# Query and key rotation in eight dealt steps, and a PSUM ring turned by one bank, in a transformer layer on one core

## The chip, the cores and the metric

The kernel runs on one core of a Trainium2 chip. It is one launch that computes a whole layer for 512 latent tokens and 128 context tokens, 640 in all. The metric is the device time of one execution in microseconds (us). The kernel before takes 1811.43 us, the median of three runs from 1809.01 to 1812.48 us.

The core has five engines with a queue each. PE multiplies matrices and writes its sums to PSUM, a memory of eight banks. DVE does arithmetic on two tensors and reductions. ACT does functions of one tensor, copies among them. POOL and SP issue most of the transfers here. Each engine works through its own queue in order and waits for the others by semaphores.

## The reference

A layer is a half-step feed-forward block, then two token mixers side by side (differential attention and a chunked linear recurrence, the mLSTM), a gated sum of the two, and a second half-step feed-forward block. The change touches the attention branch. What is computed there:

```python
dq = rmsnorm(dq.reshape(B, T, DA_HEADS, 2, DA_HEAD_DIM), p['g_qn'][l])
dk = rmsnorm(dk.reshape(B, T, DA_HEADS, 2, DA_HEAD_DIM), p['g_kn'][l])
q_att = rope_2d(dq)                                   # latent tokens only
keys  = concatenate([rope_2d(dk), k_ctx])
s  = einsum('bqhcd,bkhcd->bhcqk', q, k) * scale
pr = softmax(s)                                       # c = 0, 1
w  = pr[:, :, 0] - lam * pr[:, :, 1]
out = einsum('bhqk,bkhv->bqhv', w, v)
```

Each query and each key is a vector of 64. It is divided by its root mean square, scaled by a gain and, for the 512 latent tokens, rotated: each pair (x1, x2) becomes (x1 cos - x2 sin, x2 cos + x1 sin). The 128 context tokens get norm and gain alone, and their keys are also an output (`new_k`). There are eight heads of two vectors each, and attention has a pair of softmaxes per head.

## The kernel before, in words

The token axis lies in five tiles of 128: four of latent tokens and one of context tokens. Matrix products are in fp32r with every operand split into a high and a low part, three products for one (`mm3`). Weights come in granules of 1 MB, are loaded to `raw`, and are split by one ACT copy (`wH`, the high part) and one DVE subtraction (`wL`, the low part).

**The prelude** (from about 450 to 650 us of the span) makes the queries and keys of pair 0, that is of heads 0 and 1, and then twelve granules of gates. Its PSUM pool `ps2` has five banks under one tag, `mm`. Groups of token tiles take one bank each (`tok_group`), and each of the twelve granules takes three (X, Y and Z, in `products`). Then the pool is closed and its five banks are given to two new pools, `ps2m` with four banks and `ps2w` with one; a tile of the new pools waits until the old tile in its place has been read.

**The attention blocks** (about 684 to 1061 us) are 8 heads x 5 query tiles, in two loops in lines 2035 and 2037: head `hd`, query tile `qi`. A block does, in the order of the program:

1. `scores(qi)`: PE multiplies the query tile by all keys into the PSUM tile `sc`, and DVE takes the row minimum (`mn`);
2. `turn(qi-1)`: PE transposes the weights of the query tile before (`ps_wT`), and ACT copies them out (`wT`);
3. `soft(qi)`: ACT takes two exponentials of `sc`;
4. `aside(hd, qi, 0)`: one pending low part of a weight granule, if there is one (`fill.low()`);
5. one unit of other work for PE (`fill.units`), to cover the softmax;
6. `mix(qi)`: DVE joins the two softmaxes (`rc`, `r`, `p`);
7. `values(qi-1)`: PE multiplies the turned weights by the values (`ps_o`), and DVE scales them (`ao`);
8. in query tile 3, `pack` of the next head: ACT copies `qpk`, `kpk`, `kpk`, and DVE a subtraction `qpk`;
9. `aside(hd, qi, 1)`, perhaps a second unit of other work, and `fill.ahead()`, which loads and splits weights to come.

After the fifth block a tail turns the last query tile, transposes the next head's queries and keys (`ps_qkT`), does three units, and ends with `finish_norm` of the head's result. The transposes of that result (`ps_aT`, in `finish`) come in the first block of the next head.

The units of other work come from a queue, `fill`. A unit of a token granule makes one tile of 128 tokens; a unit of a wide pair (two granules side by side, ten units) makes half of one and uses the single bank of `ps2w`; a unit of a feature granule makes a quarter of a transposed product. The queue's order before is: values 0, keys 1, queries 1, wide values 1 and memory values 0, wide keys 2 and queries 2, memory queries 1 (feature), wide values 2, wide keys 3 and queries 3, wide values 3, then feature granules. The numbers are pairs of heads: pair 2 is heads 4 and 5. `UNITS` says how many units each block takes: 2, 1, 2, 1, 1 and three in the tail for most heads.

**What sets the order.** PE instructions stay in program order (`mm`, `tr`). For the other engines a planner runs a model of the chip and issues what it finds ready, except inside `with written():`. There each ACT or DVE instruction is chained behind the previous written one of its engine, so the written instructions of an engine form one row in the order of the program (`placed`, lines 37 to 47). Instructions outside are put between them by the planner. Steps 1, 2, 3, 4, 6, 7, 8 and `fill.ahead()` above are written.

**Norm and rotation before** (`qk_norm_rope`, line 1530) is called when the last tile of a projection of queries or keys has been copied out. It is not written: the planner puts its instructions where it finds room. It squares (ACT), sums (DVE), takes the inverse root (ACT logarithm and exponential, three small DVE instructions), multiplies (DVE), copies with halves swapped (ACT), multiplies by the sine and by the cosine table, adds, and multiplies the context tile by the gain (DVE).

Of the kernel before, what the change touches and what calls it, by code (L numbers as in the profile page):

```python
# [7 lines left out]
F32 = mybir.dt.float32  # L8
F32R = mybir.dt.float32r
BF16 = mybir.dt.bfloat16  # L10
AF = mybir.ActivationFunctionType
# [20 lines left out]
def tile_trunk(ctx: ExitStack, tc: tile.TileContext, a: dict):  # L32
# [17 lines left out]
    def act(*args, **kw):  # L50
        return placed(nc.scalar.activation(*args, **kw))  # L51

    def tt(eng, out, in0, in1, op):
        return placed(eng.tensor_tensor(out=out, in0=in0, in1=in1, op=op))  # L54
# [4 lines left out]
    def ts(out, in0, s1, op0, s2=None, op1=None):  # L59
        if s2 is None:  # L60
            placed(vec.tensor_scalar(out=out, in0=in0, scalar1=s1, scalar2=None, op0=op0))
        else:
            placed(vec.tensor_scalar(out=out, in0=in0, scalar1=s1, scalar2=s2, op0=op0, op1=op1))
# [4 lines left out]
    @contextmanager  # L68
    def written():
        was, as_written[0] = as_written[0], in_row  # L70
        yield
        as_written[0] = was
# [107 lines left out]
    def rstd_of(pool, ss, inv_n, shape, tag, bufs=1, ytag=None, ybufs=1):  # L180
        v = pool.tile(shape, F32, tag=tag + "v", name="rv", bufs=bufs)
        y = pool.tile(shape, F32, tag=ytag or tag + "y", name="ry", bufs=max(bufs, ybufs))
        t = pool.tile(shape, F32, tag=tag + "t", name="rt", bufs=bufs)
        ts(v, ss, inv_n, ALU.mult, EPS, ALU.add)
        act(t, v, AF.Ln)
        act(y, t, AF.Exp, scale=-0.5)
        newton_rsqrt(y, v, t)
        return y
# [1334 lines left out]
    def rope_place(of):  # L1523
        if not late_p:
            return rope_p[0].tile([128, 5, 256], F32, tag="pk", name="rope", bufs=2)
        return late_p[0].tile([128, 5, 256], F32, tag="rope", name="rope")

    at_rope = [None]

    def qk_norm_rope(raw, tab):  # L1530
        A, B, g = tab
        sq = rope_place("q")
        act(sq, raw, AF.Square)
        ss = rope_p[0].tile([128, 20], F32, tag="ss", name="ss", bufs=2)
        vec.tensor_reduce(out=ss, in_=sq.rearrange("p t (g d) -> p (t g) d", d=64), axis=AX.X, op=ALU.add)
        rs = rstd_of(rope_p[0], ss, 1.0 / 64, [128, 20], "qk")
        r3 = raw.rearrange("p t (g d) -> p (t g) d", d=64)
        tt(vec, r3, r3, rs[:, :, None].to_broadcast([128, 20, 64]), ALU.mult)
        sw = rope_place("k")[:, 0:4]
        at_rope[0] = act(  # L1540
            sw.rearrange("p t (b s j) -> p (t b) s j", s=2, j=16),
            raw[:, 0:4, :].rearrange("p t (b s j) -> p (t b) s j", s=2, j=16)[:, :, ::-1, :],
            AF.Copy,
        )
        s4 = sw.rearrange("p t (g d) -> p t g d", d=64)
        q4 = raw[:, 0:4, :].rearrange("p t (g d) -> p t g d", d=64)
        tt(vec, s4, s4, B[:, :, None, :].to_broadcast([128, 4, 4, 64]), ALU.mult)
        tt(vec, q4, q4, A[:, :, None, :].to_broadcast([128, 4, 4, 64]), ALU.mult)
        tt(vec, raw[:, 0:4, :], raw[:, 0:4, :], sw, ALU.add)
        p3 = raw[:, 4, :].rearrange("p (g d) -> p g d", d=64)  # L1550
        tt(vec, p3, p3, g[:, None, :].to_broadcast([128, 4, 64]), ALU.mult)

    q_tok, k_tok, v_tok = {}, {}, {}

    def project_q(pr, now=lambda f: f()):
        def make():
            q_tok[pr] = t = (ap if pr % 2 else qk).tile([128, 5, 256], F32, tag="qtok", name="q_tok")

            def evac(p, i):
                act(t[:, i, :], p, AF.Copy)  # L1560
                if i == 4:
                    now(lambda: qk_norm_rope(t, tabs[0]))

            return evac

        return a["w_dq"][pr], make

    def project_k(pr, now=lambda f: f()):
        def make():
            t = (ap if pr % 2 else qk).tile([128, 5, 256], F32, tag="ktok", name="k_tok")  # L1570
            k_tok[pr] = t

            def evac(p, i):
                act(t[:, i, :], p, AF.Copy)
                def whole():
                    qk_norm_rope(t, tabs[1])
                    nc.sync.dma_start(out=a["new_k"][:, pr * 256 : (pr + 1) * 256], in_=t[:, 4, :])

                if i == 4:
                    now(whole)  # L1580

            return evac

        return a["w_dk"][pr], make

    def project_v(pr):
        def make():
            v_tok[pr] = t = ap.tile([128, 7, 256], F32, tag="vtok", name="v_tok", bufs=2)
            nc.sync.dma_start(out=t[:, 4:6, :], in_=a["cache_v"][:, :, pr * 256 : (pr + 1) * 256])

            def evac(p, i):
                act(t[:, i if i < 4 else 6, :], p, AF.Copy)
                if i == 4:
                    nc.sync.dma_start(out=a["new_v"][:, pr * 256 : (pr + 1) * 256], in_=t[:, 6, :])

            return evac

        return a["w_dv"][pr], make
# [192 lines left out]
    def wide(*projects):  # L1791
        fill.pair([src for src, _ in projects], lambda: wide_units(psum, [make() for _, make in projects]))

    def queries_of_memory(h):
        def evac(p, mt, hf):
            t = ap.tile([128, HALF], F32, tag="stage", name="stage", bufs=2)
            act(t, p, AF.Copy, scale=0.0625)
            nc.sync.dma_start(out=mq_dram[:, 2 * h + mt, half(hf)], in_=t)
        feature(a["w_mq"][h], lambda: evac)

    def keys_of_memory(h):
        def evac(p, mt, hf):
            t = ap.tile([128, HALF], F32, tag="stage", name="stage", bufs=2)
            vec.tensor_copy(t, p)
            nc.sync.dma_start(out=mk_dram[:, 2 * h + mt, half(hf)], in_=t)
        feature(a["w_mk"][h], lambda: evac)
# [8 lines left out]
    def memory_values(h):  # L1815
        return a["w_mv"][h], lambda: v_evac(h)
# [7 lines left out]
    token(project_q(1))  # L1824
    wide(project_v(1), memory_values(0))
    projections(2)
    queries_of_memory(1)
    wide(project_v(2), memory_values(1))
    projections(3)
    wide(project_v(3), memory_values(2))  # L1830
    keys_of_memory(1)
    queries_of_memory(2)
    keys_of_memory(2)
# [85 lines left out]

    heads = [Head(hd) for hd in range(8)]  # L1920
    gates = ExitStack()
    tok_group(psum, [(w_q, i, e_q) for i in (2, 3, 4)], lambda k: None)
    G.work[0][0].load()
    with tc.issue_after(box["normed"]):
# [93 lines left out]
    def aside(hd, qi, part):  # L2018
        if hd == 0:
            for _ in range(ROWS.get((qi, part), 0)):  # L2020
                next(rows, None)
        if part == 0:
            with written():
                fill.low()
        if part == 1 and hd == 1 and qi in (1, 2):
            gate_load(qi - 1)
        if part == 0 and hd == 1 and qi in (2, 3):
            gate_cols()
# [5 lines left out]
    late = None  # L2034
    for hd in range(8):
        H = heads[hd]
        for qi in range(5):
            n = UNITS[hd][qi]
            with written():
                H.scores(qi)  # L2040
                if qi > 0:
                    H.turn(qi - 1)
                H.soft(qi)
            aside(hd, qi, 0)
            fill.units(n[0])
            with written():
                H.mix(qi)
            if late is not None:
                late()
                late = None  # L2050
            if qi > 0:
                with written():
                    H.values(qi - 1)
            if qi == 3 and hd < 7:
                with written():
                    heads[hd + 1].pack()
            aside(hd, qi, 1)
            if (hd, qi) == (0, 2):
                begin_pools()
            fill.units(n[1])  # L2060
            with written():
                fill.ahead()
        n = UNITS[hd][-1]
        with written():
            H.turn(4)
        if hd < 7:
            N = heads[hd + 1]
            N.queries()
            fill.units(n[0])
            with written():  # L2070
                H.values(4)
            H.finish_norm()
            N.keys(0)
            fill.units(n[1])
            N.keys(1)
            with written():
                fill.ahead()
            fill.units(n[2])
            late = H.finish
        else:  # L2080
            fill.eager = True
            fill.units(1)
            H.values(4)
            H.finish_norm()
            fill.drain(3)
            with written():
                H.finish()
# [547 lines left out]
```

## Time and profile before

| what | us |
|---|---|
| three runs, lowest, median, highest | 1809.01, 1811.43, 1812.48 |
| the profiled execution's own time | 1810.32 |
| its span, first to last instruction | 1808.4 |
| PE busy in the span | 1778.9 |
| DVE busy | 1346.6 |
| ACT busy | 900.2 |

The profile is of one execution. An instruction's row gives its start in us from the start of the span, its duration, engine, line, operation, the tiles it writes and reads, and shapes; in brackets stands the time for which its engine sat idle just before it, and who ended that wait. PE instructions overlap: a product of 128 x 512 starts 0.23 us after the one before it and yet is shown with about 0.4 us. So a busy PE is not a PE at its peak, and an idle time under 0.15 us gets no bracket. DVE and ACT instructions overlap by some 0.05 to 0.1 us.

### The profile page before, as it was taken

How to read it: one execution, taken by the hardware profiler on the slowest of the kernel's cores; microseconds unless marked ns; L12 is line 12 of the kernel's file. 1: busy time of each engine (PE TensorE's matmuls, PEld its weight loads, DVE VectorE, ACT ScalarE, POOL GpSimd, SP SyncE). 2: the span in 40 equal slices, each digit the busy share in tenths (PEclk: the TensorE clock that was granted, in tenths of full speed). 3: DMA queues.
4: the chain of work that ended last, by engine and by line, in shares of the span. 5: the costliest groups of instructions: out<-in, count | busy, mean ns of one | idle time of the engine just before them, and what ended most of it. 6: DMA issues, size and time to landing. Idle time of an engine off the chain costs nothing.

```text
span 1808.4 us, 29656 instructions
## 1 busy us (share of the span) xinstructions
PE 1778.9 (98%) x11950; PEld 1713.3 (95%) x11950; DVE 1346.6 (74%) x2162; ACT 900.2 (50%) x1579; POOL 41.0 (2%) x72
## 2 busy tenths in 40 slices
PE   8999999999999999999999999999999999999998
PEld 7999999999999999898889998899999999999998
DVE  6889987677988768667586447877668888897475
ACT  5654544333655456554565447562326545554432
POOL 0000000100000000000000000000000000000010
PEclk9999999999999999999999999999999999999999
DMA  8355566978245533312223335665652455557992
GB/s 325 114 198 173 185 236 220 351 223 272 84 138 183 195 129 100 110 61 69 75 72 110 106 99 197 188 244 205 217 173 77 134 173 187 203 180 272 355 311 84
DMA packets 144923, 317.85 MB, mean 176 GB/s; under 512 B 10577, under 2 KB 106577, under 8 KB 133009
## 3 DMA queue, kind: packets, MB, share of 16 engines
q1 hardware_dynamic: 133410, 270.20, 43.9%
q0 software_dynamic: 10688, 43.13, 7.4%
q10 hardware_dynamic: 688, 2.63, 0.4%
q8 instruction: 94, 1.54, 0.3%
q14 instruction: 43, 0.35, 0.1%
HBM read 243.77 MB, written 72.15 MB: 175 GB/s over the span
## 4 chain that ended last, share of the span: by engine, by line
PE 84%; DVE 8%; DMA 5%; ACT 2%; issue 1%; SPq 0%; DVEq 0%; ACTq 0%
PE ps_f L75 48%; PE ps_p L75 14%; PE ps_t L75 11%; PE sc L75 3%; PE ps_o L75 2%; PE ps_n L75 2%; DVE ww L54 2%; DMA raw_a<-in_w_ada_k 1%; PE ps_wT L78 1%; DMA P<-nm_dram 1%; PE ps_u L75 1%; PE ps_qkT L78 1%; DVE junk L814 1%; DMA raw<-in_w2b 1%; DMA a_raw<-aT_dram 1%
## 5 line engine op out<-in xcount | busy, mean ns | idle before, releaser
L75 PE MATMUL ps_f<-S,ww 128*128 128x320 f32 x2400 | 387.0, 309 | 3.2 <-DMA S<-g_dram 1.0
L75 PEld LDWEIGHTS ps_f<-S,ww 128*128 128x128 f32 x2400 | 359.8, 188 | 7.2 <-DVE ww L54 4.6
L54 DVE TENSOR_TENSOR ww<-raw,ww 128x2048 fp32r<-128x2048 f32 (+1 forms) x73 | 163.9, 2245 | 65.5 <-ACT ww L51 65.4
L75 PE MATMUL ps_f<-hm,ww 128*128 128x320 f32 x1176 | 185.6, 309 | 0.1
L75 PEld LDWEIGHTS ps_f<-hm,ww 128*128 128x128 f32 x1176 | 175.7, 188 | 0.3 <-DVE ww L54 0.3
L51 ACT ACTIVATE ww<-raw 128x2048 fp32r<-128x2048 f32 (+1 forms) x73 | 136.8, 1875 | 57.1 <-DVE raw L54 37.8
L54 DVE TENSOR_TENSOR raw<-raw 128x1024 f32<-128x1024 f32 x186 | 160.7, 864 | 2.4
L75 PE MATMUL ps_f<-hm,wB 128*128 128x320 f32 x1008 | 161.5, 309 | 0.0
L75 PE MATMUL ps_t<-wH,hH 128*128 128x256 f32 (+1 forms) x440 | 151.4, 344 | 2.9 <-DVE g_out L54 1.5
L75 PE MATMUL ps_p<-hH,wH 128*128 128x320 f32 x480 | 151.1, 315 | 1.6 <-DVE num L54 1.4
L75 PEld LDWEIGHTS ps_f<-hm,wB 128*128 128x128 f32 x1008 | 151.3, 188 | 0.0
L75 PE MATMUL ps_p<-hH,wL 128*128 128x320 f32 x480 | 148.3, 309 | 0.0
L75 PE MATMUL ps_p<-hL,wH 128*128 128x320 f32 x480 | 148.3, 309 | 0.0
L75 PE MATMUL ps_t<-wH,hL 128*128 128x256 f32 (+1 forms) x440 | 146.7, 333 | 0.9 <-DVE hL L54 0.9
L75 PE MATMUL ps_t<-wL,hH 128*128 128x256 f32 (+1 forms) x440 | 146.2, 332 | 0.0
L51 ACT ACTIVATE u<-ps_f 128x320 f32<-128x320 f32 x129 | 55.8, 433 | 157.0 <-PE ps_f L75 156.9
L51 ACT ACTIVATE wH<-raw 128x2048 fp32r<-128x2048 f32 (+1 forms) x45 | 75.4, 1683 | 48.8 <-PE ps_p L75 37.3
L54 DVE TENSOR_TENSOR wL<-raw,wH 128x2048 fp32r<-128x2048 f32 x37 | 84.6, 2286 | 19.5 <-ACT wH L51 19.3
L1674 DVE TENSOR_REDUCE mn<-sc 128x2 f32<-128x1536 f32 (+1 forms) x40 | 59.6, 1490 | 50.2 <-PE sc L75 50.0
L54 DVE TENSOR_TENSOR wB<-raw,wB 128x1024 fp32r<-128x1024 f32 x64 | 78.0, 1219 | 24.4 <-ACT wB L51 24.4
L814 DVE CUSTOM_DVE_ANT_0 junk<-raw_a,csil 128x1024 bf16<-128x1024 f32 (+1 forms) x76 | 92.5, 1217 | 2.1 <-DMA raw_a<-in_w_ada_c 1.6
L75 PEld LDWEIGHTS ps_t<-wH,hH 128*128 128x128 f32 x440 | 83.6, 190 | 11.0 <-DVE g_out L54 1.7
(306 smaller groups left out, 3595.9 us busy)
## 6 DMA issues: line engine op xcount, KB each, us to landing
g_dram<-g SPq DMA_DIRECT2D x44, 640.0 KB, 7.6
raw_a<-in_w_ada_c POOLq DMA_DIRECT2D x38, 512.0 KB, 5.1
g_dram<-g SPq DMA_DIRECT2D x24, 480.0 KB, 8.4
raw<-in_w1b SPq DMA_DIRECT2D x11, 1024.0 KB, 5.0
raw<-in_w3b SPq DMA_DIRECT2D x11, 1024.0 KB, 6.2
raw<-in_w1a SPq DMA_DIRECT2D x10, 1024.0 KB, 5.0
raw<-in_w3a SPq DMA_DIRECT2D x10, 1024.0 KB, 6.2
hm<-g_dram SPq DMA_DIRECT2D x7, 1280.0 KB, 11.8
```

The lines of the kernel that those rows point to most:

```text
L51: return placed(nc.scalar.activation(*args, **kw))
L54: return placed(eng.tensor_tensor(out=out, in0=in0, in1=in1, op=op))
L75: tc.keep_in_program_order(nc.tensor.matmul(*args, **kw))
L78: tc.keep_in_program_order(nc.tensor.transpose(*args, **kw))
L814: placed(vec.tensor_tensor_reduce(out=junk, in0=raw, in1=self.csil[:, v, :], op0=ALU.mult, op1=ALU.add, scale=1.0, scalar=0.0, accum_out=m ...
L1674: placed(vec.tensor_reduce(out=mn, in_=sv, axis=AX.X, op=ALU.min))
```

## The change

It does four things.

- `qk_norm_rope` becomes `rope_steps`, a list of eight functions: `square` (ACT), `sums` (DVE: reduction and a small scaling), `root` (two small ACT instructions), `divide` (three small DVE instructions and a product), `swap` (ACT), `by_sine` (DVE), `by_cosine` (DVE), `add` (DVE: the sum and the gain of the context tile; then the store of `new_k` for keys). The instructions are those of before. Pair 0 still runs them in one go.
- For pairs 1 to 3 the finished projection appends its list to `rotations`. A new function `rotate` runs the next step of the first list, and under some conditions also one of the second, inside `written()`, so that the steps take places in the rows of ACT and DVE. It is called in `aside` part 0 if `fill.low()` had nothing to do, in `aside` part 1 always, after the block's second units if two lists are open, and, in query tile 3 of odd heads, until nothing is left, ahead of `pack` of the next head.
- `queries_of_memory(1)`, a feature granule of four units, moves in the fill queue from behind the wide pair of keys 2 and queries 2 to behind wide values 3.
- In the prelude, ahead of the second group of queries, a PSUM tile `ps_turn` is taken from `ps2` and never used.

```diff
-    def qk_norm_rope(raw, tab):
+    def rope_steps(raw, tab, then=lambda: None):
         A, B, g = tab
...
+        def sums():
...
+            placed(vec.tensor_reduce(out=ss, in_=box.pop("sq").rearrange("p t (g d) -> p (t g) d", d=64), axis=AX.X, op=ALU.add))
+            ts(box["v"], ss, 1.0 / 64, ALU.mult, EPS, ALU.add)
+        def root():
+            act(box["t"], box["v"], AF.Ln)
+            act(box["y"], box["t"], AF.Exp, scale=-0.5)
+        def divide():
+            newton_rsqrt(box["y"], box["v"], box["t"])
+            r3 = raw.rearrange("p t (g d) -> p (t g) d", d=64)
+            tt(vec, r3, r3, box["y"][:, :, None].to_broadcast([128, 20, 64]), ALU.mult)
...
+        return [square, sums, root, divide, swap, by_sine, by_cosine, add]
+
+    def qk_norm_rope(*args):
+        for f in rope_steps(*args):
+            f()
+
+    rotations = []
+
+    def rotate():
+        if not rotations:
+            return False
+        first, second = rotations[0], rotations[1] if len(rotations) > 1 else []
+        had, left = len(first), len(second)
+        with written():
+            if not (had == 4 and left == 7):
+                first.pop(0)()
+            if left == 8 and had in (5, 6) or left in (5, 6, 7) and left >= had + 2 or left == 7 and had == 4:
+                second.pop(0)()
+            if not first:
+                rotations.pop(0)
+        return True
...
-                    now(lambda: qk_norm_rope(t, tabs[0]))
+                    if now:
+                        now(lambda: qk_norm_rope(t, tabs[0]))
+                    else:
+                        rotations.append(rope_steps(t, tabs[0]))
...
     projections(2)
-    queries_of_memory(1)
     wide(project_v(2), memory_values(1))
     projections(3)
     wide(project_v(3), memory_values(2))
+    queries_of_memory(1)
     keys_of_memory(1)
...
+    psum.tile([128, 512], F32, tag="mm", name="ps_turn")
     tok_group(psum, [(w_q, i, e_q) for i in (2, 3, 4)], lambda k: None)
...
         if part == 0:
             with written():
-                fill.low()
+                split = fill.low()
+            if not split:
+                rotate()
+        else:
+            rotate()
...
+        odd = hd % 2
...
             if qi == 3 and hd < 7:
+                while odd and rotate():
+                    pass
                 with written():
                     heads[hd + 1].pack()
             aside(hd, qi, 1)
...
             fill.units(n[1])
+            if len(rotations) > 1:
+                rotate()
             with written():
                 fill.ahead()
```

More of the change, by code (lines that the diff above doesn't have):

```diff
@@ L1528, in tile_trunk @@
     at_rope = [None]
-    def qk_norm_rope(raw, tab):
+    def rope_steps(raw, tab, then=lambda: None):
         A, B, g = tab
[L1532 to L1551, printed above, removed]
@@ new lines, in rope_steps, with square @@
+        box = {}
+        def square():
+            box["sq"] = rope_place("q")
+            act(box["sq"], raw, AF.Square)
+        def sums():
+            box["v"], box["t"], box["y"], ss = (
+                rope_p[0].tile([128, 20], F32, tag="qk" + n, name="qk" + n, bufs=2) for n in ("v", "t", "y", "ss")
+            )
+            placed(vec.tensor_reduce(out=ss, in_=box.pop("sq").rearrange("p t (g d) -> p (t g) d", d=64), axis=AX.X, op=ALU.add))
+            ts(box["v"], ss, 1.0 / 64, ALU.mult, EPS, ALU.add)
@@ new lines, in root, with swap @@
+        def root():
[5 more added lines that the diff above has]
+            tt(vec, r3, r3, box["y"][:, :, None].to_broadcast([128, 20, 64]), ALU.mult)
+        def swap():
+            box["sw"] = rope_place("k")[:, 0:4]
+            at_rope[0] = act(
+                box["sw"].rearrange("p t (b s j) -> p (t b) s j", s=2, j=16),
+                raw[:, 0:4, :].rearrange("p t (b s j) -> p (t b) s j", s=2, j=16)[:, :, ::-1, :],
+                AF.Copy,
+            )
@@ new lines, in by_sine, with by_cosine, add @@
+        def by_sine():
+            s4 = box["sw"].rearrange("p t (g d) -> p t g d", d=64)
+            tt(vec, s4, s4, B[:, :, None, :].to_broadcast([128, 4, 4, 64]), ALU.mult)
+        def by_cosine():
+            q4 = raw[:, 0:4, :].rearrange("p t (g d) -> p t g d", d=64)
+            tt(vec, q4, q4, A[:, :, None, :].to_broadcast([128, 4, 4, 64]), ALU.mult)
+        def add():
+            tt(vec, raw[:, 0:4, :], raw[:, 0:4, :], box["sw"], ALU.add)
+            p3 = raw[:, 4, :].rearrange("p (g d) -> p g d", d=64)
+            tt(vec, p3, p3, g[:, None, :].to_broadcast([128, 4, 64]), ALU.mult)
+            then()
@@ L1553, in tile_trunk, with project_q @@
     q_tok, k_tok, v_tok = {}, {}, {}
-    def project_q(pr, now=lambda f: f()):
+    def project_q(pr, now=None):
         def make():
@@ L1561, in evac, with project_k @@
                 if i == 4:
-                    now(lambda: qk_norm_rope(t, tabs[0]))
+                    if now:
+                        now(lambda: qk_norm_rope(t, tabs[0]))
+                    else:
+                        rotations.append(rope_steps(t, tabs[0]))
             return evac
         return a["w_dq"][pr], make
-    def project_k(pr, now=lambda f: f()):
+    def project_k(pr, now=None):
         def make():
@@ L1574, in evac, with store @@
                 act(t[:, i, :], p, AF.Copy)
-                def whole():
-                    qk_norm_rope(t, tabs[1])
+                def store():
                     nc.sync.dma_start(out=a["new_k"][:, pr * 256 : (pr + 1) * 256], in_=t[:, 4, :])
                 if i == 4:
-                    now(whole)
+                    if now:
+                        now(lambda: qk_norm_rope(t, tabs[1], store))
+                    else:
+                        rotations.append(rope_steps(t, tabs[1], store))
             return evac
@@ L2023, in aside @@
             with written():
-                fill.low()
+                split = fill.low()
+            if not split:
+                rotate()
+        else:
+            rotate()
         if part == 1 and hd == 1 and qi in (1, 2):
```

## The prediction

> **What bounds the kernel now.** First the page: busy times and the chain that ended last.
>
> ```profile
> PE 1778.9 (98%) x11950; PEld 1713.3 (95%) x11950; DVE 1346.6 (74%) x2162; ACT 900.2 (50%) x1579; POOL 41.0 (2%) x72
> ...
> PE 84%; DVE 8%; DMA 5%; ACT 2%; issue 1%; SPq 0%; DVEq 0%; ACTq 0%
> ```
>
> PE does its work in a fixed order and the change takes none of it away, so all that can be won is PE's idle time: 1808.4 - 1778.9 = 29.5 us of the span, 1.6%. The second view is PE's waits, longest first; these are the rows that lie in reach of the change.
>
> ```profile
> PE ps_wT L78 <- DVE p L57: 2.2, 3, 1.8
> PE ps_aT L78 <- DVE ao L54: 2.1, 2, 1.7
> ...
> PE ps_t L75 <- DVE g_out L54: 1.5, 1, 1.5
> ...
> PE ps_qkT L78 <- DVE ao L61: 1.2, 1, 1.2
> ```
>
> Together 7.0 us, 0.39% of the time. Third, the timeline says where they are and what DVE did meanwhile: heads 2 and 3 (805 to 842 us) and the first block of head 5 (931 us).
>
> ```profile
> 819.59 0.30 PE L78 MATMUL ps_wT<-ident,p 128*128 128x128 f32 x1 [1.83 <-DVE p L57]
> 826.36 0.37 PE L78 MATMUL ps_qkT<-identr,kpk 128*128 128x128 f32 x2 [1.21 <-DVE ao L61]
> 837.74 0.77 PE L78 MATMUL ps_aT<-ident,ao 128*128 128x128 f32 x5 [0.46 <-DVE ao L54]
> 931.24 0.77 PE L78 MATMUL ps_aT<-ident,ao 128*128 128x128 f32 x5 [1.68 <-DVE ao L54]
> ...
> 816.45 1.22 DVE L54 TENSOR_TENSOR k_tok<-k_tok,ropeAk 128x1024 f32<-128x1024 f32 x1
> ...
> 817.71 1.22 DVE L54 TENSOR_TENSOR k_tok<-k_tok,rope 128x1024 f32<-128x1024 f32 x1
> ...
> 819.10 0.35 DVE L57 SCALAR_TENSOR_TENSOR p<-p,r,p 128x128 f32<-128x128 f32 x1
> ```
>
> The planner put the rotation of keys 2 ahead of the last mix of head 2 (819.10), and PE waited for that mix. The other three waits have the rotations of queries 2 and keys 3 in front of the same way. These four are the stalls to be won: 1.83 + 1.21 + 0.46 + 1.68 = 5.2 us. Pair 1 is rotated in heads 0 and 1, and no PE wait for DVE stands there in the blocks.
>
> **The change part by part.** *The steps' own cost* is that of the same instructions as before; by DVE's groups in the blocks, one of each kind:
>
> ```profile
> L1535 DVE TENSOR_REDUCE ss<-rope 128x20 f32<-128x1280 f32 x6 | 8.9, 1482 | 2.2 <-ACT rope L51 2.2
> L1688 DVE RECIPROCAL rc<-sm 128x2 f32<-128x2 f32 x40 | 6.5, 163 | 40.7 <-ACT p L51 40.7
> ...
> L54 DVE TENSOR_TENSOR k_tok<-k_tok,ry 128x1280 f32<-128x1280 f32 x3 | 4.5, 1490 | 0.0
> ...
> L54 DVE TENSOR_TENSOR rope<-rope,ropeBk 128x1024 f32<-128x1024 f32 x3 | 3.7, 1221 | 0.2 <-ACT rope L51 0.2
> ...
> L54 DVE TENSOR_TENSOR k_tok<-k_tok,g_kn 128x256 f32<-128x256 f32 x3 | 1.2, 412 | 0.0
> ```
>
> ```profile
> L51 ACT ACTIVATE rope<-k_tok 128x1280 f32<-128x1280 f32 x3 | 3.8, 1279 | 0.0
> ...
> L51 ACT ACTIVATE rope<-k_tok 128x1024 f32<-128x1024 f32 x3 | 3.2, 1060 | 0.0
> ```
>
> The last two are `square` and `swap` on ACT. `sums` takes about 1.6 us of DVE, `divide` 2.1 (three instructions 0.2 us apart, then 1.49), `by_sine` and `by_cosine` 1.22 each, `add` 1.6. The row of the reciprocal shows the cover: ahead of each of 40 mixes DVE idles, 1.0 us in the mean, until the exponentials are done. A step in that place (part 0), or after the mix of a block with two units, costs nothing while it is shorter than what is left there; if that cover were gone it would delay the mix by its own 1.2 to 2.1 us.
>
> *Where the steps fall* follows from the code, by counting units and pending low parts. Keys 1 are done in the first unit of head 0, queries 1 in the last unit of block (0, 2), writing (head, query tile). Keys 1 then take all places until (0, 4), and queries 1 get five: (1, 0) parts 0 and 1, (1, 1) parts 0 and 1, (1, 2) part 1. In (1, 2) and (1, 3) part 0 goes to a low part. So `by_sine`, `by_cosine` and `add` of queries 1 are left over in (1, 3), and the loop for odd heads runs all three there, between the mix and `pack`. Keys and queries 2 come out together in (2, 2): `square` and `sums` of the keys there; in (2, 3), after `pack`, `root` of keys, `square` of queries, `divide` of keys, `sums` of queries; the other ten until (3, 2). Pair 3 does the same from (4, 2) to (5, 2), since the granule that moves away lets keys 3 come out in (4, 2) instead of the tail of head 4.
>
> *The end of head 1.* DVE, ACT and PE there now:
>
> ```profile
> 761.40 2.28 DVE L54 TENSOR_TENSOR wL<-raw,wH 128x2048 fp32r<-128x2048 f32 x1
> ...
> 764.26 1.02 DVE L57 SCALAR_TENSOR_TENSOR p<-p,r,p 128x768 f32<-128x768 f32 x1
> 765.19 0.34 DVE L61 TENSOR_SCALAR ao<-ps_o,rc 128x128 f32<-128x128 f32 x1
> ...
> 762.40 0.90 ACT L51 ACTIVATE p<-sc,mn 128x768 f32<-128x768 f32 x1
> ...
> 763.28 0.73 ACT L51 ACTIVATE qpk<-q_tok 128x640 fp32r<-128x640 f32 x1
> 763.91 1.36 ACT L51 ACTIVATE kpk<-k_tok 128x640 fp32r<-128x640 f32 x2
> ...
> 766.22 0.88 ACT L51 ACTIVATE wT<-ps_wT 128x512 f32<-128x512 f32 x2
> ...
> 768.88 1.50 PE L75 MATMUL ps_o<-v_tok,wT 128*128 128x128 f32 x12
> ```
>
> After the mix and `ao` (765.5) DVE must run 1.22 + 1.22 + 1.22 + 0.41 = 4.07 us, less some 0.3 of overlap: 769.3. Only then may ACT copy `qpk`, for it reads the rotated queries. In ACT's row stand behind it `kpk` twice and the copy `wT` of the turned weights: 769.3 + 0.7 + 1.3 + 0.9 = 772.2. PE's product with the values, now at 768.88, waits for `wT`: a new stall of 3.3 us. The last mix of the head is late by as much and is hidden behind it.
>
> *The ends of heads 2 and 4.* Head 4, which has no rotation in this place before, shows the room:
>
> ```profile
> 907.76 1.02 DVE L57 SCALAR_TENSOR_TENSOR p<-p,r,p 128x768 f32<-128x768 f32 x1
> ...
> 908.96 0.82 DVE L54 TENSOR_TENSOR qpk<-q_tok,qpk 128x640 fp32r<-128x640 f32 x1
> 909.69 0.42 DVE L1674 TENSOR_REDUCE mn<-sc 128x2 f32<-128x256 f32 x1
> ...
> 912.16 0.35 DVE L57 SCALAR_TENSOR_TENSOR p<-p,r,p 128x128 f32<-128x128 f32 x1
> ...
> 910.84 0.40 ACT L51 ACTIVATE p<-sc,mn 128x128 f32<-128x128 f32 x1
> ...
> 913.99 0.27 PE L78 MATMUL ps_wT<-ident,p 128*128 128x128 f32 x1
> ```
>
> The row minimum of block (4, 4) started at 909.69, the exponentials at 910.84, the mix ended at 912.51, and PE turned its result at 913.99. With the change `divide` and `sums` stand between `qpk` and the minimum. Their inputs come from ACT in time: `root` needs two small instructions behind `kpk`, `square` 1.28 us more. 909.7 + 2.05 + 1.55 = 913.3 for the minimum; 0.45 later the exponentials; from their start to the mix's end 912.51 - 910.84 = 1.67. That gives 915.4, 1.4 us past 913.99. A low part that now stands ahead of the mix of (4, 3) adds some 0.3 to 0.4, as in head 1, where it ended at 763.68 and the exponentials at 763.30. I take 1.7 for each of heads 2 and 4, 3.4 in all. After it DVE has `by_sine`, `divide` and `by_cosine` (1.22 + 2.1 + 1.22 = 4.5 us) ahead of the copies that PE needs in the tail; the tail's three wide units, 8.4 us by the kernel's costs, cover them, so I take nothing. Bounds for each head: 0.8, if the planner has both ready earlier, and 2.7, if the tail is late too.
>
> *The other places* (parts 0, blocks with two units) I take at nothing, by the idle time above. *The moved granule* is the same work for PE. By the costs written beside them in the kernel its units are longer than a wide one (3.3 against 2.8 us), so the single-unit block of head 2 has less cover and that of head 5 more; nothing in sum.
>
> *The PSUM ring.* At the hand-over PE waits once:
>
> ```profile
> 654.68 0.39 PE L75 MATMUL ps_t<-wH,hH 128*128 128x256 f32 x1 [1.48 <-DVE g_out L54]
> ...
> 654.14 0.48 DVE L54 TENSOR_TENSOR g_out<-ps_f,u 128x320 f32<-128x320 f32 x1
> ...
> 653.09 1.91 ACT L51 ACTIVATE wH<-raw 128x2048 fp32r<-128x2048 f32 x1 [1.06 <-PE ps_f L75]
> 654.90 0.42 ACT L51 ACTIVATE g_out<-ps_f 128x320 f32<-128x320 f32 x1
> ```
>
> The first token unit takes the bank of the last granule's Z, which DVE reads until 654.62. Turned, that bank may hold X, which was read long before (the wait of 1.5 goes), or Y, the last of all: ACT reads it until 655.32, which is 0.7 later. The rows don't say which, so I take the middle, -0.4, with both ends for the range.
>
> *The sum*: -5.2 + 3.3 + 3.4 - 0.4 = +1.1 us on the profiled execution's 1810.32 (span 1808.4 and 1.9 around it): 1811.4. That execution was 1.1 below the median of the runs, so a median of about **1812.5**. The gain that is there is paid back in other places of the same rows. The parts' own bounds (head 1: 2.3 to 3.8; heads 2 and 4: 1.6 to 5.4; the ring -1.5 to +0.7; of the 5.2 perhaps 1 stays) put the forecast between 1809 and 1816.
>
> **The rivals.**
>
> *The steps fit* (faster). If a part 0 or two is free where I count a low part, queries 1 are through before (1, 3), and steps of pairs 2 and 3 move out of the stretch between `pack` and the row minimum. Then the three new stalls vanish: 1811.43 - 5.2 - 0.4 = 1805.8. For it: DVE is busy only 74% of the span, and the 40.7 us ahead of the mixes are nearly what the six rotations of pairs 1 to 3 need, 6 x 7.7 = 46 us. Against it: a row binds whatever room there is elsewhere, and the counts come from the code.
>
> *ACT makes the single wide bank late* (slower). A wide unit can start only when ACT has copied the one before out of the only bank of `ps2w` (two copies of 0.38). In heads 1 to 4 `square` (1.28) or `swap` (1.06) stand in ACT's row near these copies. Where the planner puts the copies behind two exponentials (1.8), the step and their own 0.65, PE has only the 1.5 us of a value product as cover: 1.8 + 1.28 + 0.65 - 1.5 = 2.2 us a block, decided by whether the copy stands ahead of or behind the step. In two blocks 4.4: 1812.5 + 4.4 = 1816.9. Against it: PE's list of waits before has none for `k_tok`, `v_tok` or `stage` of a wide unit.
>
> *The clock falls after the long stall.* The first products of the kernel, 28 of 128 x 128, ran at half pace:
>
> ```profile
> 1.06 6.03 PE L75 MATMUL ps_idle<-ones 128*128 128x128 f32 x28 [1.06 <-DVE ones L128]
> ```
>
> 6.03 / 28 = 0.215 us each; the five transposes of that size at 931.24 took (0.77 - 0.27) / 4 = 0.125 each, with 0.27 for a single one at 913.99. Were PE to fall back to that pace after the 3.3 us at the end of head 1, for as long as at the start, it would lose 3.0 us: 1815.5. No idle time of PE in this trace reaches 2 us, so none shows whether 3.3 is enough. The Trainium skill, in "TensorE: Matmul & The Clock Gate", section "What's actually happening", puts the limit at an idle window of about 3.4 us and the way back at a busy one of as long; by that page the loss would be an estimated 1.7 us, and the time an estimated 1814.2.
>
> *The change does nothing where it counts*: the written places end up where the planner had them, and the stalls stay: 1811.4. Against it, the leftover steps of (1, 3) have no such place before.
>
> **How the numbers follow.** The forecast has 0.50, the steps that fit 0.23, the late bank 0.15, the fallen clock 0.06, no effect 0.06. A measurement of this kernel can tell some 0.2% from no change, 3.6 us: faster is below 1807.8, slower above 1815.1. Faster: most of the second case and 0.03 of the first, 0.23. Slower: most of the third and fourth and 0.06 of the first, 0.24. The rest, 0.53, is the same. The range for 8 in 10 reaches over the middle of the second case and that of the third: 1805.5 to 1816.9.
>
> **What would show it.** Right: no rotation ahead of the mix of block (2, 4), no long PE wait for `ao` in heads 3 and 5; a PE wait of about 3.3 us for `wT` in block (1, 4), with `q_tok<-q_tok,rope` directly ahead of `qpk` on DVE; waits for `p` of 1 to 2 us in (2, 4) and (4, 4). Wrong: no such wait in (1, 4), or new waits for ACT copies of `k_tok`, `v_tok` and `stage`. The PE row at the hand-over near 653 us settles the ring. A time below 1808 says that the steps fit; one above 1815 that something I priced at nothing is on PE's path.

## The result: 0.55% slower

| kernel | median, us | runs from, to | mean granted clock |
|---|---|---|---|
| before | 1811.34 (6 runs) | 1809.01, 1812.48 | 1.000 (profiled run) |
| after | 1820.79 (6 runs) | 1819.53, 1823.87 | 0.9957 |

The ratio is 1.0055, with a 95% interval from 1.0042 to 1.0068: about 9.5 us more. The forecast was 1812.5 us, at most 1816.9. The profiled execution of after took 1823.87 us, with a span of 1822.0; that of before took 1810.32.

First the page of after: busy times, the row of the granted clock, and the chain that ended last.

```profile
PE 1788.1 (98%) x11950; PEld 1720.5 (94%) x11950; DVE 1348.2 (74%) x2162; ACT 901.1 (49%) x1579; POOL 40.8 (2%) x72
...
PEclk9999999999999999999999999999999999999999
...
PE 84%; DVE 7%; DMA 4%; ACT 3%; issue 1%; SPq 0%; DVEq 0%; ACTq 0%
```

PE is the bound as before. But the same 11950 instructions keep it busy 1788.1 us, 9.2 more than before, and idle time grew only from 29.5 to 33.9 us. Waits alone would leave busy time as it was. So the first thing to ask is whether PE ran slower somewhere. The clock row can't answer: a slice of it is 45 us long, and a 9 stands for 90% and more.

The second view is PE's waits in after: what PE waited for, total us, times, longest.

```profile
PE ps_wT L78 <- DVE p L57: 6.0, 7, 2.5
PE ps_o L75 <- ACT wT L51: 3.9, 2, 3.4
...
PE ps_t L75 <- ACT stage L51: 1.2, 1, 1.2
...
PE ps_t L75 <- DVE g_out L54: 1.1, 1, 1.1
```

The waits for `ao` (2.1 and 1.2 us before) are gone from the list, and so is the 1.83 us wait of head 2 as it was; a longer one with another cause stands in its place. The new waits are one of 3.4 us for `wT`, two of 2.5 us for `p`, and one of 1.2 us for a copy of the wide bank. The timeline shows the new places:

```profile
759.23 0.50 PE L75 MATMUL ps_t<-wH,hH 128*128 128x512 f32 x1 [1.16 <-ACT stage L51]
...
776.39 1.01 PE L75 MATMUL ps_o<-v_tok,wT 128*128 128x128 f32 x3 [3.43 <-ACT wT L51]
...
828.77 0.33 PE L78 MATMUL ps_wT<-ident,p 128*128 128x128 f32 x1 [2.52 <-DVE p L57]
...
924.88 0.33 PE L78 MATMUL ps_wT<-ident,p 128*128 128x128 f32 x1 [2.52 <-DVE p L57]
```

These are block (1, 2), block (1, 4), and the ends of heads 2 and 4. What DVE and ACT did ahead of the 3.43 us:

```profile
769.41 1.21 DVE L54 TENSOR_TENSOR rope<-rope,ropeBq 128x1024 f32<-128x1024 f32 x1
...
770.54 1.22 DVE L54 TENSOR_TENSOR q_tok<-q_tok,ropeAq 128x1024 f32<-128x1024 f32 x1
...
772.28 1.22 DVE L54 TENSOR_TENSOR q_tok<-q_tok,rope 128x1024 f32<-128x1024 f32 x1
...
773.86 0.74 ACT L51 ACTIVATE qpk<-q_tok 128x640 fp32r<-128x640 f32 x1 [3.90 <-DVE q_tok L54]
774.50 1.35 ACT L51 ACTIVATE kpk<-k_tok 128x640 fp32r<-128x640 f32 x2
...
775.76 0.85 ACT L51 ACTIVATE wT<-ps_wT 128x512 f32<-128x512 f32 x2
```

The three leftover steps of queries 1 stand one behind the other on DVE (a subtraction `kL` of 0.68 us comes between them), ACT idles 3.90 us for them, and the copy of the turned weights is behind `qpk` and `kpk` in ACT's row.

The view that decides is the windows, cut finely around these places. Columns: stretch, its length, PE's busy time and instructions, granted clock, share of DMA, GB/s.

```profile
771.75:775.16 3.41, 1.21 (x6) 1.00 0.22 74
775.16:778.57 3.41, 2.18 (x10) 0.50 0.00 0
778.57:781.99 3.42, 3.42 (x19) 0.50 0.00 0
826.36:829.77 3.41, 1.00 (x12) 1.00 0.00 0
829.77:833.18 3.41, 3.41 (x10) 0.50 0.00 0
921.94:925.35 3.41, 0.89 (x10) 1.00 0.00 0
925.35:928.76 3.41, 3.41 (x14) 0.50 0.02 5
```

Behind each of the three long waits TensorE ran at half clock, for 6.83, 3.41 and 3.41 us. Two more such stretches of 3.41 us stand at 34.5 us, behind a DMA wait of 1.85 us in the opening, and at 1130 us, behind a wait of 1.79 us in the mLSTM. In the profile of before the mean clock over the whole span is 1.000, so it has none. Half clock costs at most half of its length: (6.83 + 4 x 3.41) / 2 = 10.2 us here, about the growth of busy time. Over the six runs of after the mean clock was 0.9957, that is up to 0.0043 x 1820 = 7.8 us each; over the 29 runs of before beside the first experiments it was 0.9987, 2.4 us. The difference is 5.4 us a run.

### The profile page after: what moved, and what is told of

It reads as the page before. It is cut to its first block, busy times and chain, and to the rows that moved or that the text cites. A ratio compares the mean times of both kernels' runs of the same rounds, so it can differ in the third digit from the quotient of the medians.

```text
span 1822.0 us, 29653 instructions
## 1 busy us (share of the span) xinstructions
PE 1788.1 (98%) x11950; PEld 1720.5 (94%) x11950; DVE 1348.2 (74%) x2162; ACT 901.1 (49%) x1579; POOL 40.8 (2%) x72
## 3 DMA queue, kind: packets, MB, share of 16 engines
q10 hardware_dynamic: 688, 2.63, 0.4%
## 4 chain that ended last, share of the span: by engine, by line
PE 84%; DVE 7%; DMA 4%; ACT 3%; issue 1%; SPq 0%; DVEq 0%; ACTq 0%
PE ps_f L75 48%; PE ps_p L75 14%; PE ps_t L75 10%; PE sc L75 2%; PE ps_o L75 2%; PE ps_n L75 2%; DVE ww L54 2%; DMA raw_a<-in_w_ada_k 1%; PE ps_qkT L78 1%; DMA P<-nm_dram 1%; PE ps_wT L78 1%; PE ps_u L75 1%; DMA raw<-in_w2b 1%; DVE junk L814 1%; DMA a_raw<-aT_dram 1%
```

## The experiments

Each ratio is against runs of the kernel before on the same chip, whose median lay between 1809.3 and 1810.0 us.

| kernel | median, us | ratio to before | 95% interval |
|---|---|---|---|
| e1_head1_early | 1813.03 | 1.0017 | 1.0008 to 1.0026 |
| e2_heads24_later | 1813.02 | 1.0019 | 1.0010 to 1.0027 |
| e3_both | 1808.00 | 0.9983 | 0.9973 to 0.9993 |
| e4_keep_clock | 1820.44 | 1.0060 | 1.0048 to 1.0072 |
| e9_keep_clock_sized | 1813.93 | 1.0026 | 1.0016 to 1.0036 |
| e10_parts_without_steps | 1804.61 | 0.9978 | 0.9969 to 0.9988 |
| e5_move_only | 1804.06 | 0.9964 | 0.9951 to 0.9977 |
| e6_turn_only | 1810.36 | 0.9999 | 0.9991 to 1.0008 |
| e12_steps_without_move | 1820.46 | 1.0057 | 1.0042 to 1.0072 |
| e8_idle_lengths | 1836.21 (one run) | | |

**Do the three stalls carry the loss?** e1 takes the leftover out of block (1, 3):

```diff
-            if len(rotations) > 1:
+            if len(rotations) > 1 or rotations and hd == 1:
                 rotate()
```

> Against the kernel after: in head 1 the rotation of queries 1 gets one more step per block (its by_sine, by_cosine and add are done by block (1,2)), so nothing is left to be drained ahead of the pack of block (1,3). Theory A (new stalls, and each makes the granted TensorE clock fall to half for about 3.4 or 6.8 us behind it): the 3.4 us wait of PE for wT in block (1,4) goes and the clock stays whole there: 6.1 us less than after, so 1814.7 us. Rival B (the stalls alone; the clock falls come by chance and would be there or elsewhere): 3.4 us less, 1817.4 us. Rival C (the loss lies in the PSUM turn or the moved granule): no change, 1820.8 us.

e2 keeps the steps away from the ends of heads 2 and 4:

```diff
-            if not split:
+            if not split and not (hd in (2, 4) and qi == 4):
                 rotate()
-        else:
+        elif not (hd in (2, 4) and qi == 3):
             rotate()
...
-            if len(rotations) > 1:
+            if (len(rotations) > 1 or rotations and hd in (3, 5)) and not (hd in (2, 4) and qi == 3):
                 rotate()
```

> Against the kernel after: heads 2 and 4 issue no step behind the units of block 3 and none in block 4, where PE idled 2.5 us twice for p; heads 3 and 5 issue one step more behind the units of each block. Theory A (stalls and the clock that falls behind them): two stalls of 2.5 us and two half-clock stretches of 1.7 us each go, 8.4 us less, and the steps that are put off may cost up to 3 us in heads 3 and 5: 1812.4 to 1815.4 us. Rival B (stalls alone): 5.0 us less at most, 1815.8 to 1818.8 us. Rival C (PSUM turn or granule): 1820.8 us.

e3 has both edits, with the extra step in every odd head (`odd` for `hd == 1` and `hd in (3, 5)`).

> Both of these edits at once: head 1 done early, and no step at the end of heads 2 and 4. Theory A: 6.1 and 5.4 to 8.4 us less than after, 1806.3 to 1809.3 us, faster than before by 2 to 5 us (the 5.2 us of rotation stalls are won and little is paid), and the granted clock 1.000 in the attention blocks. Rival B (stalls alone): 1812.4 to 1815.4 us. Rival C: 1820.8 us.

Against after's 1.0055, e1 gives back 0.0038 (6.9 us), e2 0.0036 (6.5) and e3 0.0072 (13.0). All three are near theory A's numbers, and they add up; a loss in the turn or the granule (rival C) is out. Against the stalls alone the case is weaker by time: e1 also lost the 1.16 us wait of block (1, 2), so that e3 takes 3.4 + 5.0 + 1.2 = 9.6 us of waits away, and with 3 us of interval 13.0 lies only just above it. In the waits of e1 the 3.4 us for `wT` is down to 0.5 and the two of 2.5 us are left; in those of e2 it is the other way round:

```profile
PE ps_wT L78 <- DVE p L57: 6.1, 7, 2.5
...
PE ps_o L75 <- ACT wT L51: 0.5, 1, 0.5
```

```profile
PE ps_o L75 <- ACT wT L51: 3.9, 2, 3.4
...
PE ps_wT L78 <- DVE p L57: 1.0, 5, 0.2
```

The clock went with the stalls. In e1 the half-clock stretches of the blocks stand at 825.5 and 921.1 us, behind the two stalls that it keeps; in e2 the only one stands at 773.8, behind the stall that it keeps; in e3 there is none. Taken at the same PE instruction in both traces, e1 gains 6.2 us on after at the end of head 1, of which the wait is 3.4; e2 gains 4.3 at each of its two places, of which the wait is 2.5. The put-off steps of e3 are paid with two waits of PE for a score bank: DVE does rotation steps ahead of the row minimum, the exponentials come late, and PE waits for the bank that they read.

```profile
PE sc L75 <- ACT p L51: 1.8, 2, 1.0
```

e1's own profiled execution had a stretch of 10.2 us at half clock at 385 us, in the first feed-forward block, where the code is that of before. It began behind a DMA wait of 1.9 us, and a wait of 4.0 us for a late weight granule fell into it. e1's runs go from 1808.31 to 1819.08 us. So the clock also falls at places that the change doesn't touch.

**What does the half clock cost by itself?** e4 leaves the waits and keeps TensorE running in them:

```diff
+    def keep_clock(n):
+        p = psum.tile([128, 512], F32, tag="mm", name="ps_keep")
+        for _ in range(n):
+            mm(p[:, :128], ident, ident, start=True, stop=True)
...
             if qi > 0:
+                if (hd, qi) == (1, 4):
+                    keep_clock(26)
                 with written():
                     H.values(qi - 1)
...
+        if hd in (2, 4):
+            keep_clock(18)
         with written():
             H.turn(4)
```

> The kernel after, with matmuls that nobody reads (identity by identity, 128 columns) ahead of the three products that wait: 26 in block (1,4), 18 at the end of heads 2 and 4. The waits for wT and p stay as long; TensorE only isn't idle in them. They turn the PSUM ring by three banks in all. Theory A: the granted clock stays whole behind these three places, 2.7 + 1.7 + 1.7 = 6.1 us less than after, 1814.7 us. Rival B (stalls alone): no less, 1820.8 us or up to 2 us more, as the extra matmuls take time of their own.

The clock stayed whole, but the time was that of after. This looked like rival B until the extra products were measured in its timeline: the three groups took 5.8, 4.0 and 4.0 us, 13.8 where the waits had been 8.5. They filled the waits and delayed PE by some 5.3 us more, nearly what the clock gave back. So the run by itself decided nothing. e9 has 14, 10 and 10 of them.

> e4_keep_clock again with fewer matmuls. In e4 the clock stayed whole, but the 26, 18 and 18 extra matmuls took 5.8, 4.0 and 4.0 us where the waits had been 3.4, 2.5 and 2.5: 5.4 us more than they filled, and the median came to that of after. Here 14, 10 and 10, by 0.22 us each 3.1, 2.2 and 2.2 us, which lie inside the waits. Theory A (the waits and the half clock behind them): clock whole there, 6 us less than after, ratio to before 1.001 to 1.003 (after: 1.0055). Rival B (the waits alone, half clock costs nothing as the work there waits for other engines anyway): ratio 1.0055 as after.

```profile
771.50:775.00 3.50, 3.38 (x30) 1.00 0.01 2
775.00:778.50 3.50, 3.05 (x25) 1.00 0.00 0
822.50:826.00 3.50, 3.14 (x30) 1.00 0.00 0
826.00:829.50 3.50, 3.50 (x22) 1.00 0.02 5
917.00:920.50 3.50, 3.10 (x29) 1.00 0.00 1
920.50:924.00 3.50, 3.50 (x23) 1.00 0.00 0
```

In these windows of e9 the clock is whole at all three places. The ratio is 1.0026, below after's by 0.0029 (5.2 us, give or take 3) with intervals that don't touch. The two traces say where. At the first product behind each wait e9 leads after by as much as ahead of that wait, to within 0.1 us: the extra products lie inside the waits, and PE still idles 0.3 to 0.4 us behind each group. In the 6 us behind the three waits it then gains 2.0, 1.6 and 1.5 us, 5.1 in all. The products compute nothing that is used, so this is the price of the half clock, and rival B falls. (The three extra tiles also turn the PSUM ring by three banks. That was not run by itself; one bank alone is worth nothing in e6 below.)

**What do the other two parts do?** e10 has the moved granule and the turned ring without any step: before, with

```diff
     projections(2)
-    queries_of_memory(1)
     wide(project_v(2), memory_values(1))
     projections(3)
     wide(project_v(3), memory_values(2))
+    queries_of_memory(1)
...
+    psum.tile([128, 512], F32, tag="mm", name="ps_turn")
```

> The kernel before with the two edits that have nothing to do with the steps: the granule of the queries of memory moved behind the values, and the PSUM ring turned by one bank. The prediction gives them 0 and 0.4 us less. Theory A: ratio 0.999 to 1.001, the wait of PE at the first product behind the prelude some 0.3 us shorter. Rival C (the loss of after lies in these): ratio 1.003 to 1.0055.

Neither theory had this: 0.9978, faster than before by some 4 us. The list of PE's waits has no row for `ps_aT` or `ps_qkT` any more, and that of `ps_wT` is at 0.3 us at most. The rotations are whole in this kernel, and yet all four stalls are gone that the steps were credited with. Two runs part the two edits:

> The kernel before with the moved granule alone. Before, with this edit and the turned PSUM ring, took 0.9978 of before's time and had none of the four rotation stalls, though its rotations are whole. Theory M (the move does it: the granules that come after it, and with them the whole rotations of pair 3 and the split work beside those of pair 2, lie in other places): ratio 0.997 to 0.999, and none of the waits of PE for ao in heads 2 and 4. Rival R (the turned ring does it: the transposes wait for another bank): ratio 0.999 to 1.001, with the four stalls as before.

> The kernel before with the turned PSUM ring alone. Theory M: ratio 0.999 to 1.001, the four stalls as before (1.83, 1.21, 0.46 and 1.68 us). Rival R: ratio 0.997 to 0.999, without them.

The granule does it: 0.9964 by itself, while the turned ring by itself is 0.9999 and keeps all four stalls:

```profile
821.61 0.30 PE L78 MATMUL ps_wT<-ident,p 128*128 128x128 f32 x1 [1.82 <-DVE p L57]
828.38 0.36 PE L78 MATMUL ps_qkT<-identr,kpk 128*128 128x128 f32 x2 [1.20 <-DVE ao L61]
839.77 0.77 PE L78 MATMUL ps_aT<-ident,ao 128*128 128x128 f32 x5 [0.45 <-DVE ao L54]
...
933.24 0.77 PE L78 MATMUL ps_aT<-ident,ao 128*128 128x128 f32 x5 [1.68 <-DVE ao L54]
```

DVE's timeline of e5 in the last block of head 2 shows how, beside the three rows of before in the prediction:

```profile
815.15 0.35 DVE L57 SCALAR_TENSOR_TENSOR p<-p,r,p 128x128 f32<-128x128 f32 x1
815.63 0.35 DVE L61 TENSOR_SCALAR ao<-ps_o,rc 128x128 f32<-128x128 f32 x1
815.90 1.22 DVE L54 TENSOR_TENSOR rope<-rope,ropeBk 128x1024 f32<-128x1024 f32 x1
817.03 1.22 DVE L54 TENSOR_TENSOR k_tok<-k_tok,ropeAk 128x1024 f32<-128x1024 f32 x1
```

In before the mix came at 819.10, behind the rotation rows shown in the prediction; here it comes at 815.15, ahead of them. Around it the units of the queries of memory have made way for units of a wide pair, and the planner, which is free to place the whole rotation, now puts it behind the mix. Keys 3 moved as well: they are rotated in head 4 from 904.9 us on, not at its end from 929.0 us on, so that the wait of head 5 is gone. Why the planner's model chose so can't be read from a trace.

The last run asks whether the steps win anything where the granule doesn't help: after, with the granule back in its old place.

> The kernel after with the granule of the queries of memory back at its old place, so that the steps are dealt in before's order of granules: pair 3 then falls into head 5, and its last steps are drained ahead of the pack of block (5,3) as those of queries 1 are in block (1,3). Theory S (the steps alone win the four stalls of before as well, and pay with stalls of their own, about 3.4 us at the ends of heads 1 and 5 and 2.5 at the end of head 2, each with half clock behind it): ratio 1.004 to 1.008. Rival N (the steps win nothing, the move alone won the stalls): 1.008 to 1.011, with waits of PE for ao in heads 2 to 5. Third case: the drain in head 5 finds cover and costs nothing: 1.001 to 1.003.

1.0057 lies in theory S's range. Its timeline shows that the stalls at the end of head 2 were cut only in part: the wait for `p` there is 1.56 us, not the 2.5 that theory S had, and no half clock follows it.

```profile
826.86 0.30 PE L78 MATMUL ps_wT<-ident,p 128*128 128x128 f32 x1 [1.56 <-DVE p L57]
832.95 0.36 PE L78 MATMUL ps_qkT<-identr,kpk 128*128 128x128 f32 x2 [0.54 <-DVE ao L61]
```

```profile
969.63 0.60 PE L75 MATMUL ps_o<-v_tok,wT 128*128 128x128 f32 x3 [3.49 <-ACT wT L51]
```

The leftover of pair 3 is now drained ahead of `pack` in head 5 and stops PE for 3.49 us, as queries 1 do in head 1, and half clock follows at 970.8 us, as it does at 772.8 in head 1.

So the parts don't add: the steps cost 0.0057 on before's order of granules, and 1.0055 - 0.9964 = 0.0091 (16.5 us) on the moved one; the granule gains 0.0036 with whole rotations and nothing with steps. The parts of the 16.5: waits of 3.4 + 2.5 + 2.5 + 1.2 = 9.6, and 5.2 of half clock by e9. That leaves 1.7, less than the intervals can tell from nothing. The version to keep is e5, faster than before by 0.36% (0.23 to 0.49) and than after by 0.9%.

One more kernel asks which idle lengths are followed by half clock: e8, the kernel before with a few idle maxima on DVE (2 to 8) ahead of seven mixes.

```diff
         def mix(self, qi):
             p0, p1, w, sm, rc = self.s[qi]
+            for _ in range(LATE.get((self.hd, qi), 0)):
+                tt(vec, p1[:, :w], p1[:, :w], p1[:, :w], ALU.max)
```

> The kernel before with 2 to 8 extra maxima of a tile with itself on DVE (the values stay as they are) ahead of the mix of seven blocks, one in each of seven heads, so that PE idles there for lengths between some 0.5 and 6 us. It is made to find which idle lengths are followed by a stretch of half clock. If the clock falls only behind idle time of 3.4 us and more, the 2.5 us waits of after were followed by half clock by chance; if a 2.5 us wait is enough, every idle time here of 2.5 us or more is followed by one stretch of 3.4 us at half clock, and those of about 3.4 us and more by one or two.

PE idled once each for 2.63, 2.96, 3.59 and 4.18 us behind them. Behind the other three mixes it idled for less than 2 us. Half clock followed the first, the second and the last of the four, not the third, nor the shorter ones. It is taken up at the end.

## Why the prediction was wrong

*Four rotation stalls, -5.2.* They are gone from after as forecast. The steps win part of that by themselves: in e12, without the moved granule, the waits in heads 3 and 5 are gone, and the two at the end of head 2 are 1.56 and 0.54 us. But they weren't needed for it: e5 removes all four with the granule alone and whole rotations. The prediction's remark that the granule lets keys 3 come out in head 4 was right, but it priced the move at nothing and never asked what whole rotations would do there.

*End of head 1, +3.3.* Right in place and order. That the size, 3.43, is so near is partly luck: the planner put a row that the sum doesn't have, the subtraction `kL` for the cached context keys (0.68 us at 771.68), among the leftover steps, and the first product with the values (776.39) starts before both copies of `wT` are done (776.61), which the sum had it wait for.

*Heads 2 and 4, +1.7 each.* Right place, too small: 2.52 each. The steps that were counted between `qpk` and the row minimum are there, and so is their length. DVE at the end of head 2:

```profile
822.36 0.69 DVE L54 TENSOR_TENSOR kL<-ck,kH 128x512 fp32r<-128x512 f32 x1 [0.42 <-ACT kH L51]
...
823.61 1.49 DVE L54 TENSOR_TENSOR k_tok<-k_tok,qky 128x1280 f32<-128x1280 f32 x1
825.01 1.48 DVE L1543 TENSOR_REDUCE qkss<-rope 128x20 f32<-128x1280 f32 x1
...
826.62 0.42 DVE L1726 TENSOR_REDUCE mn<-sc 128x2 f32<-128x256 f32 x1
...
828.36 0.35 DVE L57 SCALAR_TENSOR_TENSOR p<-p,r,p 128x128 f32<-128x128 f32 x1
```

From the minimum's start to the mix's end (828.71) it is 2.1 us, as the prediction's 0.45 + 1.67. What the sum lacks is the first row: between `qpk`, which ends at 821.95, and the first small instruction of `divide` at 822.97, DVE waits 0.42 us for ACT's copy `kH` of the cached context keys and does the subtraction `kL`, 1.0 us together. In before the planner had that subtraction behind the minimum (at 910.25 in head 4). The 0.3 that was added for a late `qpk` was not there: `qpk` ends 0.94 us after PE began to turn the mix of query tile 3 (821.01), in before 0.95. So 1.4 + 1.0 = 2.4 of the 2.5 is accounted for. That 2.5 lies within the bound of 2.7 is luck, for the bound was set for a late tail.

*The other places, nothing.* Block (1, 2) cost 1.16 us. It is the rival of the late wide bank, in one block: ACT has two exponentials, `swap` and the copies in the order that the rival described, and the wait's releaser is `stage`. It was priced at 2.2 a block.

*The ring, -0.4.* In the profiled pair the wait fell from 1.5 to 1.1 us, within 0.1 of the middle that was taken. That is luck: without the turned ring the same wait is 1.48 (before), 1.26 (e5) and 1.34 us (e8), and with it 1.13 to 1.48 us over nine profiles. No effect of the ring shows there, nor in time (e6).

*The fallen clock*, rated 0.06 and priced at 3.0 us, in one place. This is the step that failed: the sum puts the clock behind the new stalls at nothing. By the prediction's steps with the waits of the profiled pair it is -5.2 + 3.4 + 5.0 + 1.2 - 0.4 = +4.0, or 1815.4 on the median; the 5.2 us that e9 measures for the half clock behind the three waits bring it to 1820.6, and 1820.79 was measured. (So close a match is more than the 3 us of e9's interval allow to claim.) The case was thought of, with the right sign and nearly the right price for head 1: 6.2 - 3.4 = 2.8 against 3.0. By the two paces beside it, 0.215 and 0.125 us for a product, 28 products lose 2.5 us and not 3.0. But the case was weighed for the 3.3 us stall alone, and the two at the ends of heads 2 and 4 were given no clock at all. The rule that was weighed beside it, an idle window of about 3.4 us in the Trainium skill, "TensorE: Matmul & The Clock Gate", section "What's actually happening", read as a length of idle time, doesn't hold here: 2.52 us was enough twice. The profile of before had no idle time of PE above 1.85 us, so it could not give the limit; then a stall of 2.5 us should have been priced from both sides, with and without a fall of the clock.

The rival of the steps that fit was wrong for this kernel. e3, where they nearly fit, shows what it would have been worth: 1808.0, where it said 1805.8. e5 gets to 1804.1 without the steps.

## What to carry to other kernels

In this kernel a stall of PE has two prices: its own length, and, where some 2 us of idle time lie close together (the last section says how close), up to half of a 3.4 us stretch of half clock behind it, or of two. Idle time that is spread thinly has only the first. Before writing places by hand for a long chain of steps, see whether an independent piece of work beside it can be moved, and leave the chain to the planner: here one moved line alone was faster than both kernels. Work left over and drained ahead of something that gates another engine's row costs its full length.

## What the runs showed that was not expected

The half-clock stretches lie on a fixed grid of 3.413 us within an execution. In after they begin at 34.5, 775.2, 829.8, 925.3 and 1130.1 us: the distances are 217.0, 16.0, 28.0 and 60.0 times 3.413 us. What decides, as far as these traces show, is then not the length of an idle time but how much of it falls into one cell of that grid. The windows of e8, cut along its grid, show it with idle times of 2.96, 3.59 and 4.18 us:

```profile
852.49:855.90 3.41, 0.45 (x5) 1.00 0.00 0
855.90:859.32 3.42, 3.42 (x12) 0.50 0.00 0
999.26:1002.67 3.41, 1.53 (x9) 1.00 0.41 125
1002.67:1006.08 3.41, 1.69 (x13) 1.00 0.00 0
1006.08:1009.50 3.42, 3.42 (x27) 1.00 0.34 38
1057.29:1060.70 3.41, 0.35 (x2) 1.00 0.57 219
1060.70:1064.12 3.42, 2.30 (x10) 0.50 0.00 0
1064.12:1067.53 3.41, 3.41 (x15) 0.50 0.00 0
```

The 3.59 us of idle time fell half into one cell and half into the next, 1.9 and 1.7 us each, and the clock stayed whole, though 2.5 us within one cell was always followed by half clock. In the twelve traces here, all fourteen cells at full clock that had 1.91 us or more of PE's idle time were followed by a cell at half clock, none of the cells between 1.3 and 1.5 us was, and between 1.5 and 1.9 us it went both ways. A half-clock cell that itself held about 1.0 us or more of idle time was followed by another (1060.70 here, 775.16 in after), one with 0.4 us or less was not. The limit lies thus near half a cell; where exactly was not tried. Where the grid lies changes from run to run, so the same stall costs more or less by chance.
